# Retention state of the samples: key times value moved to ScalarE, decay and addition fused on VectorE, one more state tile

## Chip, core and metric

One core of one Trainium2 chip runs the whole program in one launch. The metric is device time in microseconds (us); three runs of the kernel before were timed, and one further execution was taken with the hardware profiler. Engines are named as in the profile: PE (TensorE), PEld (its weight loads), DVE (VectorE), ACT (ScalarE), POOL (GpSimd), SP (SyncE, which only issues transfers here).

## What is computed

One inference step of a decoder layer for 512 prompt tokens and 8 samples of one token each: RMS norm, one wide input projection, a gated MLP branch, a retention branch with 4 heads, an output projection and a feed-forward block. The change touches the retention state of the samples. Per head (key width 256, value width 512) and sample the reference computes, with c = 1 for a single token:

```
S_new = S * gamma + k^T v          # state, 256 x 512 per sample and head
o     = q S_new                    # output of the sample
```

`gamma` is one number per head, `S` comes from memory (`state_ret`) and `S_new` goes back (`new_ret_sample`).

## The kernel before

The program is one long stream of matrix products on PE. All weights come through `load_to` (line 200: quarter blocks of 256 KB, on SP's queue, three raw blocks deep), are split into a high and a low part by ACT (`wh`, line 232) and DVE (`wl`, line 234), four halves ahead of their use (`LA = 4`), and are multiplied in line 259, three products for each. Everything else is written as generators ("tasks") that advance by one step in each `micro()`; `half` calls `micro()` once for each of its four groups of six products. So the order of instructions on every engine, and of the transfers on SP's and POOL's queues, is set by this counting, and each engine works in that order.

The four heads (lines 951 to 970) each project keys, queries, values and gate, and run beside it `steps` (retention of the prompt in four chunks, lines 792 to 833: `Sh` by ACT, `Sl` by DVE, both read by PE in line 807), `o_norm` (line 777, with a power on POOL, line 784) and `samples` (line 869). `samples` works on 16 tiles per head, each 128 partitions (8 samples times 16 key rows) by 512 values:

- rows of q, k and v of the samples are copied by ACT into `srow` (tag "os", lines 879 to 884), stored by POOL to a scratch in memory (line 885) and read back spread over the partitions as `qp`, `kp` and `vp` (lines 890 to 892, POOL's queue);
- `sp_load(i)` (line 864) loads state tile i on SP's queue into one of 4 buffers; three are loaded ahead of the loop, and tile i + 3 is asked for at the end of pass i;
- pass i: ACT multiplies the tile by gamma in place (line 898); one step later DVE adds key times value (line 900) and POOL stores the result (line 901); one step later DVE adds it, weighted with the query, to `so` (lines 904, 906). A pass comes every `st["gap"]` steps, which differs by head and stage (`GAPS`).

A load into a buffer waits on SP until the store of the tile that had the buffer before has landed, and the weight loads behind it on SP's queue wait too. After the loop, `so` is split (line 910), summed over the key rows by PE (lines 913, 914), normed into `os_` (tag "os", lines 917 to 923), transposed (line 930) and added to the head's result.

The scratch tiles of `tmp()` (line 282, 4 buffers of 128 x 520) are used at the same time by the values (line 759), the gate (line 447 through `scaled`) and the branch gate `gb_task` (line 973).

Of the kernel before, what the change touches and what calls it, by code (L numbers as in the profile page):

```python
# [9 lines left out]
F32 = mybir.dt.float32  # L10
R = mybir.dt.float32r
AF = mybir.ActivationFunctionType
ALU = mybir.AluOpType
# [3 lines left out]
P = 128  # L17
DM = 1024
SEQ = 512
NS = 8  # L20
# [3 lines left out]
DV = 512  # L24
# [43 lines left out]
def trunk_kernel(ctx: ExitStack, tc: tile.TileContext, t: dict, o: dict):  # L68
# [5 lines left out]
    V, S, PE, G = nc.vector, nc.scalar, nc.tensor, nc.gpsimd  # L74
# [42 lines left out]
    def has(*keys):  # L117
        return lambda: all(k in done for k in keys)
# [154 lines left out]
    def x_tile():  # L273
        return ps_x.tile([P, 4, 128], F32, tag="x", name="xps")

    def item(label, x2, need=None, ps=None):
        ps = mm_tile() if ps is None else ps
        half(ps, label, x2, 0, True, False, need)
        half(ps, label, x2, 4, False, True, need)
        return ps  # L280

    def tmp():
        return base.tile([P, 2, HC], F32, tag="tmp", bufs=4, name="tmp")

    def tmp4():
        r = base.tile([P, 2 * HC], F32, tag="m4", bufs=2, name="tmp4")
        return r[:, :512].rearrange("p (a b) -> p a b", a=4)

    def hilo(oh, ol, src):

        S.activation(out=oh, in_=src, func=AF.Copy)
        yield
        V.tensor_tensor(out=ol, in0=src, in1=f32(oh), op=ALU.subtract)  # L293
# [69 lines left out]
    for k in range(8):  # L363
        if k in (2, 4):
# [3 lines left out]
                               op0=ALU.mult, op1=ALU.subtract)  # L368
# [15 lines left out]
    def rsqrt_mean(dst, src, scale, n=P):  # L384
        V.tensor_scalar(out=dst, in0=src, scalar1=scale, scalar2=EPS, op0=ALU.mult, op1=ALU.add)
        G.tensor_tensor(out=dst, in0=dst, in1=neghalf[:n, :dst.shape[-1]], op=ALU.pow)
# [266 lines left out]
    hp = hs.enter_context(tc.tile_pool(name="hp", bufs=1))  # L653
# [17 lines left out]
    def rope_first(ps):  # L671
        a, b = rot(), rot()
        V.tensor_tensor(out=a, in0=ps[:, :, :HC], in1=cosr, op=ALU.mult)
        V.tensor_tensor(out=b, in0=ps[:, :, :HC], in1=sinr, op=ALU.mult)  # L674
        return a, b
# [8 lines left out]
    def make_head(h):  # L684
        H = Head()
        g = gam[h]
# [176 lines left out]

        def sp_load(i):
            if i < 16:
                H.sp[i] = hp.tile([P, DV], F32, tag="sp", bufs=4, name="sp")
                nc.sync.dma_start(out=H.sp[i], in_=sview[:, :, i, :])

        def samples():

            yield has(*([("rs", h - 1)] if h else []), *[("vs", h, e) for e in range(4)])
            yield 3
            for j in range(2):
                pt = x_tile()
                for k in range(4):
                    PE.transpose(pt[:NS, k, :], H.smp[:, 4 * j + k, :], ident)
                pf = pt[:NS].rearrange("p a b -> p (a b)")
                yield
                srow = hp.tile([NS, 512], F32, tag="os", bufs=2, name="srow")
                if j == 0:  # L880
                    S.copy(out=srow[:, 0:256], in_=pf[:, 0:256])
                    S.mul(out=srow[:, 256:512], in_=pf[:, 256:512], mul=DK ** -0.5)
                else:
                    S.copy(out=srow, in_=pf)
                G.dma_start(out=row_d[h][:, 512 * j:512 * (j + 1)], in_=srow)
            qp = hp.tile([P, 16], F32, tag="qp", bufs=2, name="qp")
            kp = hp.tile([P, 16], F32, tag="kp", bufs=2, name="kp")
            vp = hp.tile([P, DV], F32, tag="vp", name="vp")
            so = hp.tile([P, DV], F32, tag="so", name="so")
            G.dma_start(out=qp, in_=row_d[h][:, 0:256].rearrange("s (b i) -> s b i", i=16))  # L890
            G.dma_start(out=kp, in_=row_d[h][:, 256:512].rearrange("s (b i) -> s b i", i=16))
            G.dma_start(out=vp, in_=row_d[h][:, 512:1024].unsqueeze(1).to_broadcast([NS, 16, DV]))
            for i in range(3):
                sp_load(i)
            yield 12
            for i in range(16):
                sp = H.sp.pop(i)
                S.mul(out=sp, in_=sp, mul=float(g))  # L898
                yield
                V.scalar_tensor_tensor(out=sp, in0=vp, scalar=kp[:, i:i + 1], in1=sp, op0=ALU.mult, op1=ALU.add)  # L900
                G.dma_start(out=oview[:, :, i, :], in_=sp)  # L901
                yield
                if i == 0:
                    V.tensor_scalar(out=so, in0=sp, scalar1=qp[:, 0:1], scalar2=None, op0=ALU.mult)
                else:
                    V.scalar_tensor_tensor(out=so, in0=sp, scalar=qp[:, i:i + 1], in1=so, op0=ALU.mult, op1=ALU.add)
                yield st["gap"] - 2
                sp_load(i + 3)
            soh, sol = (hp.tile([P, DV], R, tag=tag, bufs=n, name="so2") for tag, n in (("vp", 1), ("sp", 4)))
            yield from hilo(soh, sol, so)  # L910
            yield 11 if h == NH - 1 else 7
            po = x_tile().rearrange("p a b -> p (a b)")
            PE.matmul(po[:NS, :], lhsT=sel, rhs=soh, start=True, stop=False)
            PE.matmul(po[:NS, :], lhsT=sel, rhs=sol, start=False, stop=True)
            yield
            ss = hp.tile([P, 1], F32, tag="ss", bufs=2, name="ss_s")
            os_ = hp.tile([NS, DV], F32, tag="os", bufs=2, name="os_")
            S.activation(out=os_, in_=po[:NS], func=AF.Square, accum_out=ss[:NS])
            S.copy(out=os_, in_=po[:NS])
            yield 3  # L920
            rsqrt_mean(ss[:NS], ss[:NS], 1.0 / DV, NS)
            yield 2
            S.activation(out=os_, in_=os_, func=AF.Copy, scale=ss[:NS])
            yield has(*[("r", h, e) for e in range(4)])
            yield
            rh, rl = rT[h]
            pt = x_tile()
            pv = pt[:, 0, :32].rearrange("p (e s) -> p e s", e=4)
            for e in range(4):
                PE.transpose(pv[:, e, :], os_[:, 128 * e:128 * (e + 1)], ident[:NS, :NS])  # L930
            yield
            rs = tmp4()[:, 0, :32].rearrange("p (e s) -> p e s", e=4)
            for hh in range(2):
                z = rs[:, :, 4 * hh:4 * hh + 4]
                V.tensor_tensor(out=z, in0=pv[:, :, 4 * hh:4 * hh + 4], in1=H.sgs[:, :, hh], op=ALU.mult)
            yield
            for hh in range(2):
                yield from hilo(rh[:, :, hh, 256:HC], rl[:, :, hh, 256:HC], rs[:, :, 4 * hh:4 * hh + 4])
            done.add(("rs", h))
# [11 lines left out]
    for h in range(NH):  # L951
        H = make_head(h)
        st["gap"] = GAPS[h][0]
        a, b = rope_first(item(f"k{h}_0", X))
# [3 lines left out]
        a, b = rope_first(item(f"q{h}_0", X))  # L958
# [395 lines left out]
```

## Time and profile before

| | us |
|---|---|
| three timed runs | 1127.29, 1132.49, 1132.52 |
| their median | 1132.49 |
| the profiled execution, its own time | 1129.06 |
| its span, first to last instruction | 1127.3 |
| PE busy in the span | 1106.0 (98%) |
| DVE busy | 774.0 (69%) |
| ACT busy | 544.6 (48%) |
| POOL busy | 90.0 (8%) |
| granted TensorE clock, mean over the span | 0.996 of full |

How to read it: the profiled execution's time exceeds its span by 1.8 us, which lies outside of the instructions. PE's busy share counts time in which a product is under way; what is left, about 21 us, holds the start, the end and the waits between. The views used below are the page's list of engines, who waited for whom, instructions in order of time, groups of instructions by line and shape, and busy times in given windows.

### The profile page before, as it was taken

How to read it: one execution, taken by the hardware profiler on the slowest of the kernel's cores; microseconds unless marked ns; L12 is line 12 of the kernel's file. 1: busy time of each engine (PE TensorE's matmuls, PEld its weight loads, DVE VectorE, ACT ScalarE, POOL GpSimd, SP SyncE). 2: the span in 40 equal slices, each digit the busy share in tenths (PEclk: the TensorE clock that was granted, in tenths of full speed). 3: DMA queues.
4: the chain of work that ended last, by engine and by line, in shares of the span. 5: the costliest groups of instructions: out<-in, count | busy, mean ns of one | idle time of the engine just before them, and what ended most of it. 6: DMA issues, size and time to landing. Idle time of an engine off the chain costs nothing.

```text
span 1127.3 us, 22375 instructions
## 1 busy us (share of the span) xinstructions
PE 1106.0 (98%) x8954; PEld 1085.4 (96%) x8954; DVE 774.0 (69%) x1384; ACT 544.6 (48%) x999; POOL 90.0 (8%) x148
## 2 busy tenths in 40 slices
PE   9999999999999999999999999999999999999996
PEld 8999999999999899999998999999999999999996
DVE  6567833464895379557864877769868767767765
ACT  6465523245555544554455444456544444544541
POOL 0100000001211111111012121000000000000000
PEclk9999999999999999999999999999999999999998
DMA  8423243431666078428561686652323323323302
GB/s 294 132 76 95 80 129 98 128 103 50 165 200 207 21 201 248 143 51 229 153 196 38 199 269 219 189 170 76 113 76 113 113 76 113 109 80 103 99 25 76
DMA packets 112616, 148.08 MB, mean 131 GB/s; under 512 B 13752, under 2 KB 81528, under 8 KB 112512
## 3 DMA queue, kind: packets, MB, share of 16 engines
q1 hardware_dynamic: 97696, 118.75, 34.2%
q0 software_dynamic: 12336, 24.72, 7.7%
q10 hardware_dynamic: 2480, 3.19, 0.8%
q8 instruction: 70, 1.15, 0.4%
q14 instruction: 34, 0.28, 0.1%
HBM read 121.16 MB, written 25.43 MB: 130 GB/s over the span
## 4 chain that ended last, share of the span: by engine, by line
PE 81%; issue 5%; DVE 5%; DMA 4%; ACT 2%; POOL 1%; SPq 0%; ACTq 0%; DVEq 0%; POOLq 0%
PE mm L259 58%; PE bA L1171 6%; PE bB L1171 4%; PE xps L807 2%; PE bD L1171 2%; PE bC L1171 2%; PE st_ps L813 2%; DMA sp<-in_state_ret 1%; DMA raw<-in_w_in 1%; DVE wl L234 1%; PE mm L1142 1%; DVE sp L900 1%; PE xps L771 1%; ACT wh L232 1%; PE bA L1282 1%
## 5 line engine op out<-in xcount | busy, mean ns | idle before, releaser
L232 ACT ACTIVATE wh<-raw 128x512 fp32r<-128x512 f32 x333 | 209.6, 631 | 296.6 <-PE mm L259 233.5
L234 DVE TENSOR_TENSOR wl<-raw,wh 128x512 fp32r<-128x512 f32 x333 | 228.3, 687 | 95.0 <-ACT wh L232 94.0
L259 PE MATMUL mm<-xh,wh 128*128 128x260 f32 x1264 | 260.7, 287 | 2.9 <-DVE rot L674 1.2
L259 PE MATMUL mm<-xl,wh 128*128 128x260 f32 x1264 | 254.2, 283 | 0.3 <-DVE xl L367 0.3
L259 PE MATMUL mm<-xh,wl 128*128 128x260 f32 x1264 | 254.2, 283 | 0.0
L259 PEld LDWEIGHTS mm<-xh,wh 128*128 128x128 f32 x1264 | 195.7, 189 | 6.9 <-ACT wh L232 1.4
L259 PEld LDWEIGHTS mm<-xl,wh 128*128 128x128 f32 x1264 | 194.6, 188 | 0.6 <-DVE xl L367 0.5
L259 PEld LDWEIGHTS mm<-xh,wl 128*128 128x128 f32 x1264 | 194.7, 188 | 0.0
L259 PE MATMUL mm<-ah,wh 128*128 128x260 f32 x576 | 116.0, 283 | 0.0
L259 PE MATMUL mm<-al,wh 128*128 128x260 f32 x576 | 115.9, 283 | 0.0
L259 PE MATMUL mm<-ah,wl 128*128 128x260 f32 x576 | 115.7, 282 | 0.0
L259 PEld LDWEIGHTS mm<-ah,wl 128*128 128x128 f32 x576 | 88.8, 188 | 0.0
L259 PEld LDWEIGHTS mm<-al,wh 128*128 128x128 f32 x576 | 88.7, 188 | 0.1
L259 PEld LDWEIGHTS mm<-ah,wh 128*128 128x128 f32 x576 | 88.5, 188 | 0.0
L1179 DVE TENSOR_TENSOR x<-x,mm 128x520 f32<-128x520 f32 x56 | 38.8, 694 | 37.9 <-PE mm L259 37.9
L900 DVE SCALAR_TENSOR_TENSOR sp<-vp,kp,sp 128x512 f32<-128x512 f32 x64 | 47.8, 747 | 15.5 <-ACT sp L898 15.4
L901 POOL DMA_DIRECT2D out_new_s<-sp x64 | 39.0, 610 | 224.8 <-DVE sp L900 211.5
L234 DVE TENSOR_TENSOR wl<-sums,wh 128x512 fp32r<-128x512 f32 x60 | 41.3, 689 | 19.8 <-ACT wh L232 19.3
L232 ACT ACTIVATE wh<-sums 128x512 fp32r<-128x512 f32 x60 | 37.7, 629 | 33.6 <-PE mm L259 28.2
L259 PE MATMUL mm<-rl,wh 128*128 128x260 f32 x256 | 52.0, 284 | 0.6 <-DVE rl L293 0.6
L447 DVE TENSOR_TENSOR tmp<-mm,rb 128x520 f32<-128x520 f32 x37 | 25.8, 697 | 38.6 <-PE mm L259 38.6
L259 PE MATMUL mm<-rh,wh 128*128 128x260 f32 x256 | 51.6, 283 | 0.3 <-DVE ld L1007 0.3
(362 smaller groups left out, 2161.8 us busy)
## 6 DMA issues: line engine op xcount, KB each, us to landing
raw<-in_w_in SPq DMA_DIRECT2D x158, 256.0 KB
sp<-in_state_ret SPq DMA_DIRECT2D x64, 256.0 KB
out_new_s<-sp POOLq DMA_DIRECT2D x64, 256.0 KB, 5.6
raw<-in_w_up SPq DMA_DIRECT2D x64, 256.0 KB
raw<-in_w_down SPq DMA_DIRECT2D x64, 256.0 KB
raw<-in_w_proj_ret SPq DMA_DIRECT2D x32, 256.0 KB
raw<-in_w_proj_gm SPq DMA_DIRECT2D x16, 256.0 KB
raw<-in_w_out SPq DMA_DIRECT2D x16, 256.0 KB
```

Of the source, the lines that this page charges most:

```text
L232: S.activation(out=wh, in_=src, func=AF.Copy)
L234: V.tensor_tensor(out=wl, in0=src, in1=f32(wh), op=ALU.subtract)
L259: PE.matmul(ps[:, hh, :HC], lhsT=w[:, j, :], rhs=x[:, k, hh, :], start=(first and q == 0), stop=(last and q == 2))
L447: V.tensor_tensor(out=z, in0=ps[:, :, :HC], in1=rb, op=ALU.mult)
L771: PE.transpose(pt[:, c, :], z[:, hh, off:off + 128], ident)
L807: PE.matmul(po, lhsT=a, rhs=b, start=(n == 0), stop=(n == len(mms) - 1))
L813: PE.matmul(st_ps[:, d, :], lhsT=a[:, c, ks], rhs=b[:, c, :], start=(c == 0 and n == 0), stop=(c == 3 and n == 2), skip_group_check=True)
L900: V.scalar_tensor_tensor(out=sp, in0=vp, scalar=kp[:, i:i + 1], in1=sp, op0=ALU.mult, op1=ALU.add)
L901: G.dma_start(out=oview[:, :, i, :], in_=sp)
L1142: PE.matmul(ps[:, hh, :HC], lhsT=w[:, j, :], rhs=x[:, j, 2 * kh + hh], start=(kh + j + n == 0), stop=(kh == 1 and j == 3 and n == 2))
L1171: PE.matmul(ps, lhsT=w[:, k, :], rhs=x, start=(first and k + n == 0), stop=(k == 3 and n == 2), skip_group_check=True)
L1179: V.tensor_tensor(out=x1[:, m], in0=x1[:, m], in1=ps[:, :, :HC], op=ALU.add)
```

## The change

In each of the 64 passes ACT now computes key times value into a scratch tile `kv` from `tmp()` (scale `kp[:, i:i+1]`, one value per partition), without touching the state tile; DVE then does decay and addition in one operation on the loaded tile, with gamma as an immediate. The state tiles get 5 buffers in place of 4; the tiles with tag "os" get 1 in place of 2.

```diff
         def sp_load(i):
             if i < 16:
-                H.sp[i] = hp.tile([P, DV], F32, tag="sp", bufs=4, name="sp")
+                H.sp[i] = hp.tile([P, DV], F32, tag="sp", bufs=5, name="sp")
...
-                srow = hp.tile([NS, 512], F32, tag="os", bufs=2, name="srow")
+                srow = hp.tile([NS, 512], F32, tag="os", bufs=1, name="srow")
...
             for i in range(16):
+                kv = tmp()[:, :, 0:256]
+                S.activation(out=kv, in_=vp.rearrange("p (a b) -> p a b", a=2), func=AF.Copy, scale=kp[:, i:i + 1])
+                yield
                 sp = H.sp.pop(i)
-                S.mul(out=sp, in_=sp, mul=float(g))
-                yield
-                V.scalar_tensor_tensor(out=sp, in0=vp, scalar=kp[:, i:i + 1], in1=sp, op0=ALU.mult, op1=ALU.add)
+                V.scalar_tensor_tensor(out=sp, in0=sp, scalar=float(g), in1=kv, op0=ALU.mult, op1=ALU.add)
...
-            soh, sol = (hp.tile([P, DV], R, tag=tag, bufs=n, name="so2") for tag, n in (("vp", 1), ("sp", 4)))
+            soh, sol = (hp.tile([P, DV], R, tag=tag, bufs=n, name="so2") for tag, n in (("vp", 1), ("sp", 5)))
...
-            os_ = hp.tile([NS, DV], F32, tag="os", bufs=2, name="os_")
+            os_ = hp.tile([NS, DV], F32, tag="os", bufs=1, name="os_")
```

Every engine keeps its instructions in the same places; what changes is the operands and what each instruction waits for. The first place is ACT in the second head (head 1), the first passes over the state. Names in brackets are semaphores: DMAHW those of transfers from SP's queue, DMASW those from POOL's. Before:

```order
L898 ACTIVATE sp<-sp 128x512 [waits DMAHW3_49,DMASW6_49]
L898 ACTIVATE sp<-sp 128x512 [waits DMAHW4_49,DMASW7_49]
L947 COPY pbacc<-mm 128x520 [waits PE_49]
L232 ACTIVATE wh<-raw 128x512 [waits DMAHW7_49,DMAHW6_49]
L898 ACTIVATE sp<-sp 128x512 [waits DMAHW5_49,DMASW0_49]
L947 COPY pbacc<-mm 128x520 [waits PE_49]
L232 ACTIVATE wh<-raw 128x512
L898 ACTIVATE sp<-sp 128x512 [waits DMAHW0_49,DMASW5_49]
```

And now, at the same place:

```order
L898 ACTIVATE tmp<-vp,kp 128x2x256 [waits DMASW5_49,DMASW4_49]
L898 ACTIVATE tmp<-vp,kp 128x2x256
L948 COPY pbacc<-mm 128x520 [waits PE_49]
L232 ACTIVATE wh<-raw 128x512 [waits DMAHW7_49,DMAHW6_49]
L898 ACTIVATE tmp<-vp,kp 128x2x256
L948 COPY pbacc<-mm 128x520 [waits PE_49]
L232 ACTIVATE wh<-raw 128x512
L898 ACTIVATE tmp<-vp,kp 128x2x256
```

ACT's operation of the pass waited for the load of its state tile (DMAHW); now only the first of a head waits, for `vp` and `kp`. The wait for the load stands at DVE's operation of the pass (line 901 of the new program).

The second place is SP's queue in the same head: the first loads of state tiles among the weight loads. Before, and then now:

```order
L867 DMA sp<-in_state_ret 128x1x512 [waits DMAHW0_49,DMASW5_49,PE_49]
L200 DMA raw<-in_w_in 128x2x256 [waits DMAHW1_49,DVE_49]
L200 DMA raw<-in_w_in 128x2x256 [waits DMAHW2_49]
L867 DMA sp<-in_state_ret 128x1x512 [waits DMAHW3_49,DMASW7_49,DVE_49]
L200 DMA raw<-in_w_in 128x2x256 [waits DMAHW4_49]
L867 DMA sp<-in_state_ret 128x1x512 [waits DMAHW5_49,DMASW0_49,DVE_49]
```

```order
L867 DMA sp<-in_state_ret 128x1x512 [waits DMAHW0_49,DMASW0_49]
L200 DMA raw<-in_w_in 128x2x256 [waits DMAHW1_49,DVE_49]
L200 DMA raw<-in_w_in 128x2x256 [waits DMAHW2_49]
L867 DMA sp<-in_state_ret 128x1x512 [waits DMAHW3_49,DMASW4_49,PE_49]
L200 DMA raw<-in_w_in 128x2x256 [waits DMAHW4_49]
L867 DMA sp<-in_state_ret 128x1x512 [waits DMAHW5_49,DMASW7_49,DVE_49]
```

These are the loads of tiles 3, 4 and 5. Tile 4 waited for the store of this head's tile 0 (DMASW7); now tile 5 does, and tile 4 waits only for what the head before left.

The third place is ACT in the third head (head 2), where the second row is copied into the one buffer that is left:

```order
 L882 ACTIVATE srow<-xps 8x256
-L884 COPY srow<-xps 8x512 [waits PE_49,Activation_49]
+L884 COPY srow<-xps 8x512 [waits DMASW0_49,PE_49,Activation_49]
```

The copy now also waits until the store of the first row has landed (DMASW0); the same stands in the other heads.

## Rows read from the trace of the kernel before

**Rows 1.** The page: busy time of PE (us, share of the span, instructions), and the shares of the chain that ended last, by engine.

```profile
PE 1106.0 (98%) x8954; PEld 1085.4 (96%) x8954; DVE 774.0 (69%) x1384; ACT 544.6 (48%) x999; POOL 90.0 (8%) x148
PE 81%; issue 5%; DVE 5%; DMA 4%; ACT 2%; POOL 1%; SPq 0%; ACTq 0%; DVEq 0%; POOLq 0%
```

**Rows 2.** Who PE waited for, whole span: us in total, times, longest us.

```profile
PE xps L807 <- DVE Sl L824: 1.7, 1, 1.7
PE xps L913 <- ACT wh L232: 1.3, 1, 1.3
PE xps L930 <- ACT os__8296 L923: 1.2, 1, 1.2
PE mm L259 <- DVE rot L674: 1.2, 1, 1.2
...
PE mm L259 <- DVE tmp L447: 0.5, 1, 0.5
```

**Rows 3.** Windows of 6 us in head 1: stretch, then busy us (and instructions) of PE, PEld, DVE, ACT, POOL, then granted clock, DMA share, GB/s.

```profile
390.00:396.00 6.00, 6.00 (x52) 6.00 (x52) 3.61 (x6) 4.03 (x8) 1.78 (x3) 1.00 0.22 55
...
402.00:408.00 6.00, 6.00 (x53) 6.00 (x52) 1.50 (x2) 0.80 (x2) 0.61 (x1) 1.00 0.79 261
...
426.00:432.00 6.00, 4.80 (x40) 4.62 (x39) 6.00 (x10) 3.21 (x6) 0.60 (x1) 1.00 0.92 257
...
450.00:456.00 6.00, 4.85 (x42) 4.64 (x40) 5.91 (x12) 3.12 (x7) 1.03 (x2) 1.00 0.58 189
```

**Rows 4.** ACT in order of time, head 1, its operation of passes 4 and 5: start us, us, what, [idle before it, and who ended it].

```profile
403.70 0.63 ACT L898 ACTIVATE sp<-sp 128x512 f32<-128x512 f32 x1 [3.10 <-DMA sp<-in_state_ret]
407.83 0.63 ACT L898 ACTIVATE sp<-sp 128x512 f32<-128x512 f32 x1 [3.50 <-DMA sp<-in_state_ret]
```

**Rows 5.** DVE in order of time, the same stretch: its operation of passes 4, 5 and 9, and the evacuation that PE waited for at 428 us.

```profile
404.37 0.75 DVE L900 SCALAR_TENSOR_TENSOR sp<-vp,kp,sp 128x512 f32<-128x512 f32 x1 [3.03 <-ACT sp L898]
...
408.50 0.75 DVE L900 SCALAR_TENSOR_TENSOR sp<-vp,kp,sp 128x512 f32<-128x512 f32 x1 [2.59 <-ACT sp L898]
...
421.71 0.75 DVE L900 SCALAR_TENSOR_TENSOR sp<-vp,kp,sp 128x512 f32<-128x512 f32 x1 [0.77 <-ACT sp L898]
...
428.48 0.69 DVE L674 TENSOR_TENSOR rot<-mm,sinr 128x520 f32<-128x520 f32 x1
```

**Rows 6.** SP's queue in order of time: the last weight loads before the loop of head 1, and the loads of state tiles 4 and 5.

```profile
361.07 0.89 SPq L200 DMA_DIRECT2D raw<-in_w_in  x2
397.88 0.62 SPq L867 DMA_DIRECT2D sp<-in_state_ret  x1
...
399.60 0.63 SPq L867 DMA_DIRECT2D sp<-in_state_ret  x1
```

**Rows 7.** POOL in order of time: the store of state tile 0 of head 1.

```profile
393.68 0.64 POOL L901 DMA_DIRECT2D out_new_s<-sp  x1 [3.16 <-DVE sp L900]
```

**Rows 8.** Waits over the whole span, of SP's queue, of ACT and of DVE: us in total, times, longest us.

```profile
SPq L867 <- DMA out_new_s<-sp: 256.0, 50, 35.9
ACT sp L898 <- DMA sp<-in_state_ret: 23.8, 13, 4.8
DVE sp L900 <- ACT sp L898: 15.4, 10, 3.3
```

**Rows 9.** Groups of instructions by line and shape: count | busy us, mean ns of one | idle before. The first two are the operations of the pass, the third is ACT with a scale per partition from SBUF to SBUF, the last is DVE's same operation with an immediate in place of a value per partition.

```profile
L900 DVE SCALAR_TENSOR_TENSOR sp<-vp,kp,sp 128x512 f32<-128x512 f32 x64 | 47.8, 747 | 15.5 <-ACT sp L898 15.4
L898 ACT ACTIVATE sp<-sp 128x512 f32<-128x512 f32 x64 | 39.6, 621 | 23.8 <-DMA sp<-in_state_ret 23.8
L788 ACT ACTIVATE ob<-ob,ss 128x512 f32<-128x512 f32 x14 | 10.0, 715 | 0.0
L1123 DVE SCALAR_TENSOR_TENSOR tmp<-tmp,rb 128x520 f32<-128x520 f32 x30 | 20.8, 694 | 0.0
```

**Rows 10.** Around PE's wait on `Sl` in head 1: POOL's store of the first row, ACT's copy of the second and POOL's load of `vp`, in order of time, and the window in which PE waited (columns as in Rows 3).

```profile
370.37 0.59 POOL L885 DMA_DIRECT2D row_d<-srow  x1 [5.35 <-ACT srow L882]
374.76 0.56 ACT L884 COPY srow<-xps 8x512 f32<-8x512 f32 x1
379.64 0.59 POOL L892 DMA_DIRECT2D vp<-row_d  x1 [2.23 <-issue]
380.00:400.00 20.00, 18.20 (x125) 16.84 (x125) 10.61 (x18) 12.09 (x24) 4.42 (x8) 0.91 0.23 59
```

**Rows 11.** The same place in head 2, in order of time: POOL's store of the first row, ACT's copy of the second, POOL's load of `vp`, DVE's second half of `Sl`, and PE's product that reads it; and the least, median and largest time from issue to landing of the stores of line 885.

```profile
475.28 0.59 POOL L885 DMA_DIRECT2D row_d<-srow  x1 [14.91 <-ACT srow L882]
475.56 0.58 ACT L884 COPY srow<-xps 8x512 f32<-8x512 f32 x1 [0.56 <-PE xps L876]
480.31 0.59 POOL L892 DMA_DIRECT2D vp<-row_d  x1 [1.65 <-PE st_ps L813]
483.07 0.69 DVE L824 SCALAR_TENSOR_TENSOR Sl<-st_ps,Sh 128x512 fp32r<-128x512 f32 x1 [0.67 <-ACT Sh L822]
485.67 0.40 PE L807 MATMUL xps<-Sl,q 128*128 128x512 f32 x1
DMA to landing us min/median/max: 1.8/1.9/3.5
```

**Rows 12.** The end of the last head's samples: ACT in order of time, and the window around it (columns as in Rows 3).

```profile
682.17 0.63 ACT L232 ACTIVATE wh<-raw 128x512 fp32r<-128x512 f32 x1 [1.21 <-DMA raw<-in_w_proj_ret]
679.00:685.00 6.00, 6.00 (x51) 5.80 (x49) 5.14 (x10) 3.21 (x6) 1.33 (x1) 1.00 0.96 362
```

## Prediction, before the changed kernel was run

> **What bounds the kernel now.** I read the page first. PE is busy for 1106.0 of 1127.3 us and makes up 81% of the chain [rows 1], so no edit on ACT or DVE pays for itself; it can only give back time in which PE stands still, about 21 us with the start and the end. Next the list of whom PE waits for: in the part with the four heads the waits are few and short, 1.7, 1.3, 1.2, 1.2 and 0.5 us [rows 2]. That is the whole stake of this change, and the rest of the reading asks which of these waits hang on the samples' state.
>
> Three of them do, by way of DVE. In head 1 the passes over the state come closest together. ACT sits for 3.10 and 3.50 us before its operation in passes 4 and 5, each time until the state tile has landed [rows 4]; DVE, which comes after ACT in the pass, then sits idle for 3.03 and 2.59, and once more 0.77 in pass 9, 6.4 us in all [rows 5]. Between 402 and 408 us DVE is busy for only 1.50 of 6 us; afterwards it works off a backlog, 6.00 of 6 us busy from 426 to 432, where PE loses 1.2, and 5.91 from 450 to 456, where PE loses another 1.15 [rows 3]. The evacuation that PE waited for at 428 us starts at 428.48, with no idle time before it [rows 5]: DVE is late, not held up there. So PE's waits on `tmp` (0.5), `rot` (1.2) and, through the split weights, on `wh` (1.3) are the bill for DVE's idle time 20 to 50 us earlier: 3.0 us [rows 2].
>
> Why were the tiles late? SP's queue stands still from 361.96 to 397.88 us, on the load of tile 4 [rows 6]. The store of tile 0 was issued at 393.68 [rows 7], so it took 4.2 us until SP could go on. The load of tile 4, issued at 397.88, holds ACT until 403.70 (5.8 us), that of tile 5, issued at 399.60, until 407.83 (8.2 us) [rows 4, 6]. Such waits of SP on stores sum to 256.0 us in 50 cases, the longest 35.9 [rows 8]. Meanwhile the transfer engines idle: DMA share 0.22 from 390 to 396, 0.79 and more afterwards [rows 3].
>
> **The change, part by part.**
>
> *Fifth buffer.* Tile 4 of a head no longer waits for a store of the same head. In head 1 its load goes out in SP's idle stretch, and DVE's 3.03 us go. Tile 5 then waits for the store of tile 0 and goes out at about 397.9 in place of 399.6. If it needs the same 8.2 us it lands at 406.1; DVE, now 3.0 us earlier, is ready for it at about 402.9 (408.50 - 2.59 - 3.0 [rows 5]), and waits 3.2 us. DVE's idle time falls from 6.4 to between 3.2 and 4.0, so DVE gets to its backlog 2.4 to 3.2 us earlier. Each of the three waits of PE (0.5, 1.2, 1.3) is shorter than that, so I take all three off: **-3.0 us**. The bounds are 0 (the loads land no earlier) and -3.0.
>
> *Who waits for the load.* ACT's 23.8 us in 13 waits [rows 8] end. The load is now awaited by DVE, and behind it on DVE stand weight splits and evacuations; but DVE waited for ACT in the same place already (15.4 us in 10 cases [rows 8]), and the tile no longer has to pass through 0.62 us of ACT first. Nothing new is behind the wait: 0 us.
>
> *Durations.* ACT's operation gets a scale per partition; the nearest row takes 715 ns against 621, so 64 x 0.094 = 6.0 us more of ACT. DVE's gets an immediate; the nearest row takes 694 ns for 520 values against 747 for 512, so 64 x 0.053 = 3.4 us less of DVE [rows 9]. ACT is 48% busy [rows 1] and loses its waits; its cover is the four weight halves split ahead. Head 1 has 16 of the 64 passes, 0.8 us less of DVE in the backlog, which only secures the first term. On PE: 0.
>
> *Scratch tiles.* 64 more tiles go through the 4 buffers of `tmp()`. ACT may now wait for DVE to have read the `kv` of some passes before. In the branch gate's stage a buffer can also be held until a 260 KB tile is stored, but ACT has stood for up to 4.8 us on a state tile [rows 8], and of PE's waits on ACT none exceeds 1.3 [rows 2]. 0 us, nothing to gain, bounded above by the next item.
>
> *One row buffer.* The copy of the second row waits for the store of the first. That store, issued at 475.28 in head 2, needs 1.8 to 1.9 us [rows 11], so the copy moves from 475.56 to about 477.15, 1.6 us. Behind it on POOL come the second store, the loads of `qp`, `kp`, `vp` and then a power that DVE waits for ahead of `Sl`. DVE's second half of `Sl` ends at 483.07 + 0.69 = 483.8, and PE's product that reads it starts at 485.67: slack 1.9 us, 0.3 more than the delay [rows 11]. In head 1 exactly this chain already costs the wait of 1.7 us on `Sl` [rows 2], after which the granted clock fell to its lower level (mean 0.91 over 20 us, so 20 x 0.09 = 1.8 us lost) [rows 10]; there the copy starts 4.4 us behind the issue of the first store and does not move. Likeliest 0; bounds 0 and +3.5 (one more such event, 1.7 + 1.8).
>
> *The end.* In the last head PE's 1.2 us on `os_` follow a weight block that landed 1.21 us late, in a window with a DMA share of 0.96 [rows 2, 12]. SP gets to that block earlier, but the transfer engines are full. Bounds 0 and -1.2; I take **-0.5**, nearer to nothing, because of the full engines.
>
> *Sum:* -3.0 - 0.5 = **-3.5 us**, or 1129.06 - 3.5 = 1125.6 for the profiled execution. That execution lies 3.4 us below the median of the runs (1132.49), and the four executions known (1127.29, 1129.06, 1132.49, 1132.52) show two levels that nothing here explains. I apply the sum to their middle, (1129.06 + 1132.49) / 2 = 1130.8, and forecast **1127.3 us**, 0.46% below the median. About 0.5%, 5.7 us, is what a measurement of this kernel can tell from no change: under 1126.8 would be faster, over 1138.2 slower.
>
> A rule that speaks against the largest term: the Trainium skill, "DMA: Bandwidth & Descriptors", section "Issuing engines are not separate DMA queues", says that all transfers run on the same 16 engines and interleave, whoever issues them. By that rule a load issued 1.7 us earlier into a share of 0.79 to 0.92 lands hardly earlier; the trace agrees in that the load of tile 5 took longer than that of tile 4. By the rule alone the sum would be near 0; by the rows it is -3.5, since tile 4's load moves into the idle stretch.
>
> **Rivals.**
>
> *A. The forecast*, DVE earlier in head 1: 1127.3, own range 1123 to 1132. For it: the idle time stands right ahead of the backlog.
>
> *B. The transfers bind.* Stores and loads of 512 KB per pass beside the weights keep the engines at 0.8 to 0.9 [rows 3]; loads are issued earlier and land when they did. Then DVE's idle time only moves, and the time stays at 1130.8. Against it: the share of 0.22 before the loop, into which one load per head fits. The rule of the Trainium skill named above would make it this case.
>
> *C. More comes back.* Also the 1.2 us at the end and the event of head 1 (1.7 + 1.8 [rows 2, 10]) go, because transfers are spread better: 3.0 + 1.2 + 3.5 = 7.7 less, 1123.1. Against it: that event hangs on POOL's `vp` load, which the change does not touch; for it: the 3 to 5 us between the runs may be such events.
>
> *D. The row buffer makes it slower.* If in heads 0 and 2 the store of the row takes over 0.3 us longer than its median (3.5 is the maximum shown [rows 11]), the chain behind it misses its slack, PE waits and the clock falls, as in head 1: 2 x (1.7 + 1.8) = 7.0 more. With nothing gained elsewhere that is 1132.49 + 7.0 = 1139.5, slower. Against it: both heads need to miss it, on top of no gain.
>
> That the change doesn't do what it says can be left out: the waits stand in the order of instructions.
>
> **How the numbers follow.** A 0.53, B 0.20, C 0.17, D 0.10. A lies just above the line of 1126.8, so I give 0.20 of it to faster and 0.33 to no difference; with C, faster is 0.37; with B, no difference is 0.53; slower is D, 0.10. The range reaches from C's side, 1121.5, to 1134.0, which is B at the higher of the two levels; D and the far end of C are left out.
>
> **What would show it.** Right: ACT has no wait on a state load; DVE's waits at line 901 in head 1 sum to under 4.5 us; PE's waits from 410 to 460 us sum to under 0.8 where they were 3.0; SP does not stand still on tile 4 but on tile 5. B: DVE idle there for 6 us as before, with the same waits of PE. D: a wait of PE for `Sl` of over 1 us in head 0 or 2, and a granted clock under 1.00 there. Wrong altogether would be a new wait of PE of over 2 us that ends on ACT's `kv` or on a scratch tile.

## The result, and the profile of the changed kernel

The changed kernel takes 1121.49 us (median of 12 runs, 1118.84 to 1124.08); the kernel before, timed beside it, 1127.45 (12 runs, 1124.95 to 1132.52). The ratio is 0.9944, 95% interval 0.9926 to 0.9961: 6.3 us off 1127.45 by the ratio (4.4 to 8.3 by the interval), 6.0 by the medians. So the gain is real, but whether it exceeds the 0.5% that the prediction drew as its line, the interval leaves open. The forecast was 1127.3 with a range from 1121.5 to 1134.0; the result lies 5.8 us below the forecast and 0.01 us below the range.

The profiled executions are 1129.06 us (span 1127.3) and 1121.07 us (span 1119.4). The page of the changed kernel, busy time of the engines and the shares of the chain that ended last:

```profile
PE 1103.7 (99%) x8954; PEld 1084.0 (97%) x8954; DVE 770.4 (69%) x1384; ACT 549.8 (49%) x999; POOL 88.3 (8%) x148
...
PE 94%; issue 2%; DVE 2%; DMA 1%; ACT 1%; POOL 0%; SPq 0%; ACTq 0%; DVEq 0%; POOLq 0%
```

Against [rows 1], PE's busy time fell by 2.3 us and its idle time from 21.3 to 15.7, by 5.6: together the 7.9 us between the spans. The 2.3 are not fewer products. They are mostly the stretch that ran before at the lower clock, 1.8 us [rows 10]. Whom PE waits for now, whole span (us in total, times, longest us):

```profile
PE bB L1237 <- DVE dg L1232: 2.4, 1, 2.4
PE mm L259 <- ACT xh L366: 1.2, 1, 1.2
PE ps_w L344 <- DVE ones L337: 1.1, 1, 1.1
PE xps L876 <- ACT ob L781: 0.7, 1, 0.7
```

All five waits of [rows 2], on `Sl`, `wh`, `os_`, `rot` and `tmp`, 5.9 us, are gone; what heads the list lies at the end, at the start and between heads. (From line 900 of the kernel before on, the changed kernel's numbers are one higher.) Head 1 by windows, columns as in [rows 3], first the four stretches shown there, then the one of [rows 10]:

```profile
390.00:396.00 6.00, 6.00 (x52) 6.00 (x52) 5.35 (x10) 4.35 (x9) 1.85 (x3) 1.00 0.38 86
402.00:408.00 6.00, 6.00 (x53) 6.00 (x52) 3.94 (x8) 1.95 (x4) 1.20 (x2) 1.00 0.83 252
426.00:432.00 6.00, 6.00 (x53) 6.00 (x52) 5.96 (x12) 3.63 (x6) 0.60 (x1) 1.00 0.94 260
450.00:456.00 6.00, 6.00 (x52) 5.96 (x51) 3.44 (x9) 5.20 (x12) 0.56 (x1) 1.00 0.80 234
380.00:400.00 20.00, 19.86 (x149) 18.40 (x148) 12.09 (x21) 14.45 (x27) 4.46 (x8) 1.00 0.34 90
```

PE is busy for 6.00 of 6 in each of the four. DVE does 3.94 us of work from 402 to 408 where it did 1.50, and is through with its backlog by 450 (3.44 where it was 5.91). The last row has the full clock and no wait on `Sl`. SP's queue in the changed kernel, the load of tile 4, then of tiles 5 and 6, and behind them DVE's operation of the pass, passes 4, 5 and 6:

```profile
362.80 0.62 SPq L867 DMA_DIRECT2D sp<-in_state_ret  x1
...
395.35 0.63 SPq L867 DMA_DIRECT2D sp<-in_state_ret  x1
...
397.06 0.63 SPq L867 DMA_DIRECT2D sp<-in_state_ret  x1
```

```profile
398.74 0.69 DVE L901 SCALAR_TENSOR_TENSOR sp<-sp,tmp 128x512 f32<-128x512 f32 x1
...
401.34 0.69 DVE L901 SCALAR_TENSOR_TENSOR sp<-sp,tmp 128x512 f32<-128x512 f32 x1 [1.11 <-DMA sp<-in_state_ret]
...
405.36 0.69 DVE L901 SCALAR_TENSOR_TENSOR sp<-sp,tmp 128x512 f32<-128x512 f32 x1 [2.06 <-DMA sp<-in_state_ret]
```

Tile 4 is asked for 35 us earlier than in [rows 6], in SP's idle stretch, and pass 4 finds it there; SP now stands still on tile 5. Passes 5 and 6 still wait, 3.2 us in all where three passes waited 6.4 [rows 5]. Who waits over the whole span, and the two operations of the pass by line and shape (columns as in [rows 8, 9]):

```profile
SPq L867 <- DMA out_new_s<-sp: 225.4, 43, 31.4
...
ACT srow L884 <- DMA row_d<-srow: 7.2, 2, 3.9
...
DVE sp L901 <- ACT tmp L898: 4.8, 5, 1.9
...
DVE sp L901 <- DMA sp<-in_state_ret: 3.2, 2, 2.1
...
ACT tmp L898 <- DMA gb_d<-tmp: 2.5, 1, 2.5
```

```profile
L898 ACT ACTIVATE tmp<-vp,kp 128x512 f32<-128x512 f32 x64 | 45.3, 711 | 2.5 <-DMA gb_d<-tmp 2.5
...
L901 DVE SCALAR_TENSOR_TENSOR sp<-sp,tmp 128x512 f32<-128x512 f32 x64 | 43.8, 685 | 8.1 <-ACT tmp L898 4.8 <-DMA sp<-in_state_ret 3.2
```

ACT waits for no state load any more, once for a scratch tile (2.5 us) and twice for the row buffer (7.2); none of these reaches PE.

The last head, which the prediction gave one short paragraph, shows the same picture as head 1. The kernel before, DVE in order of time:

```profile
657.34 0.75 DVE L900 SCALAR_TENSOR_TENSOR sp<-vp,kp,sp 128x512 f32<-128x512 f32 x1 [1.26 <-ACT sp L898]
...
663.25 0.75 DVE L900 SCALAR_TENSOR_TENSOR sp<-vp,kp,sp 128x512 f32<-128x512 f32 x1 [3.29 <-ACT sp L898]
...
673.11 0.75 DVE L900 SCALAR_TENSOR_TENSOR sp<-vp,kp,sp 128x512 f32<-128x512 f32 x1 [1.30 <-ACT sp L898]
```

That is 5.9 us of DVE's time lost to late state tiles, 12 to 28 us ahead of PE's wait at 685.4 us. In the changed kernel no pass of this head waits for a load; the two that wait at all wait for ACT (3.3 us). Where the DMA share of 0.96 stood [rows 12], the changed kernel has:

```profile
679.00:685.00 6.00, 6.00 (x51) 6.00 (x52) 3.62 (x9) 2.10 (x5) 0.73 (x2) 1.00 0.31 98
```

The program is about 7 us ahead by then, and the last state load goes out 11.2 us earlier (654.22 against 665.44), so the transfers are done some 4 us earlier against PE's work as well.

### The profile page after: what moved, and what is told of

Its sections match the earlier page's. It is cut to its first block, busy times and chain, and to the rows that moved or that the text cites. A ratio compares the mean times of both kernels' runs of the same rounds, so it can differ in the third digit from the quotient of the medians.

```text
span 1119.4 us, 22317 instructions
## 1 busy us (share of the span) xinstructions
PE 1103.7 (99%) x8954; PEld 1084.0 (97%) x8954; DVE 770.4 (69%) x1384; ACT 549.8 (49%) x999; POOL 88.3 (8%) x148
## 4 chain that ended last, share of the span: by engine, by line
PE 94%; issue 2%; DVE 2%; DMA 1%; ACT 1%; POOL 0%; SPq 0%; ACTq 0%; DVEq 0%; POOLq 0%
PE mm L259 69%; PE bA L1172 6%; PE bB L1172 4%; PE xps L807 2%; PE bD L1172 2%; PE bC L1172 2%; PE st_ps L813 2%; PE mm L1143 1%; PE xps L771 1%; PE xps L853 1%; DMA xT<-in_xT 1%; PE bA L1283 1%; PE ps_v L259 1%; DVE x L1251 0%; PE bB L1283 0%
## 5 line engine op out<-in xcount | busy, mean ns | idle before, releaser
L259 PE MATMUL mm<-rh,wl 128*128 128x260 f32 x256 | 51.5, 282 | 0.0
```

What stands on the lines that cost most here:

```text
L259: PE.matmul(ps[:, hh, :HC], lhsT=w[:, j, :], rhs=x[:, k, hh, :], start=(first and q == 0), stop=(last and q == 2))
```

## Experiments

Every kernel below was timed side by side with the kernel before, on one chip, and its ratio is to that; experiments 7 and 8 are single profiled executions.

### 1. The fifth tile alone

```diff
-                H.sp[i] = hp.tile([P, DV], F32, tag="sp", bufs=4, name="sp")
+                H.sp[i] = hp.tile([P, DV], F32, tag="sp", bufs=5, name="sp")
-                srow = hp.tile([NS, 512], F32, tag="os", bufs=2, name="srow")
+                srow = hp.tile([NS, 512], F32, tag="os", bufs=1, name="srow")
...
```

> The kernel before with 5 state tiles and one row buffer, its operations as before (ACT scales the state tile in place, DVE adds key times value). Theory 'buffers' (the waits of PE in head 1 come from the slot cycle of store and load): 3 to 5 us faster than before, DVE's idle time ahead of line 900 from 390 to 460 us falls from 6.4 to about 3.5, and PE's waits there from 3.0 to under 0.8. Theory 'ACT freed' (what counted is that ACT no longer stands on a state load): within 1.5 us of before, PE's waits there still over 2.

Measured: 1120.68 us (1119.47 to 1123.52), ratio 0.9946 [0.9931, 0.9961], the same as the whole change. Waits over the span:

```profile
ACT sp L898 <- DMA sp<-in_state_ret: 12.5, 6, 3.1
...
DVE sp L900 <- ACT sp L898: 7.6, 9, 1.5
```

Against [rows 8] ACT's wait on loads is halved, DVE's too (2.9 us of it in head 1, where it was 6.4), and of PE's five waits none is left. So the buffers bring the whole gain, as far as the intervals can tell. Five tiles with two row buffers were not tried: the second row buffer is the space that the fifth tile takes, 512 values in each partition.

### 2. The operations alone

```diff
             for i in range(16):
+                kv = tmp()[:, :, 0:256]
+                S.activation(out=kv, in_=vp.rearrange("p (a b) -> p a b", a=2), func=AF.Copy, scale=kp[:, i:i + 1])
+                yield
                 sp = H.sp.pop(i)
-                S.mul(out=sp, in_=sp, mul=float(g))
-                yield
-                V.scalar_tensor_tensor(out=sp, in0=vp, scalar=kp[:, i:i + 1], in1=sp, op0=ALU.mult, op1=ALU.add)
+                V.scalar_tensor_tensor(out=sp, in0=sp, scalar=float(g), in1=kv, op0=ALU.mult, op1=ALU.add)
```

> The new operations alone (ACT key times value into scratch, DVE decay and addition), with 4 state tiles and two row buffers as before. 'Buffers': within 1.5 us of before, DVE now idle itself on the loads of tiles 4 and 5 for 5 us or more in all, PE's waits in head 1 at 2 us or more. 'ACT freed': 3 us or more faster, PE's waits there under 0.8.

Measured: 1125.53 us (1122.32 to 1129.69), ratio 0.9992 [0.9978, 1.0007], no difference. DVE now waits for the loads itself, 6.3 us in head 1, and PE still waits there for `rot` and at line 914, 1.8 us in all (I had expected 2 or more). The profiled execution has no wait on `Sl`. Waits over the span, of DVE and then of PE:

```profile
DVE sp L901 <- DMA sp<-in_state_ret: 12.9, 7, 2.3
```

```profile
PE xps L914 <- DVE tmp L747: 1.0, 1, 1.0
PE mm L259 <- DVE rot L674: 0.8, 1, 0.8
```

Moving the wait from ACT to DVE, the longer operation on ACT and the shorter one on DVE are together worth nothing that shows: between 2.5 us less and 0.8 more, by the interval.

### 3. The row buffer alone

```diff
-                srow = hp.tile([NS, 512], F32, tag="os", bufs=2, name="srow")
+                srow = hp.tile([NS, 512], F32, tag="os", bufs=1, name="srow")
...
-            os_ = hp.tile([NS, DV], F32, tag="os", bufs=2, name="os_")
+            os_ = hp.tile([NS, DV], F32, tag="os", bufs=1, name="os_")
```

> The kernel before with one row buffer in place of two, nothing else. If the row buffer is hidden, as predicted: within 1.5 us of before, ACT's second row copy 1.6 us later in heads 0 and 2 and no new wait of PE. If it costs: a wait of PE for Sl of over 1 us in head 0 or 2 and 3.5 us more. If it was what freed the second row's store (which landed in 3.5 us before and in 1.8 after): the second store lands in 1.8 us in all heads, the wait of 1.7 us on Sl in head 1 is gone, and 3 us less.

Measured: 1127.27 us (1124.64 to 1133.29), ratio 0.9998 [0.9984, 1.0012], no difference. ACT does wait for the row's store (4.7 us in 2 cases), and no wait of PE on `Sl` follows in heads 0 and 2. The profiled execution was the longest of them, and it shows what a long execution with four tiles consists of. Windows of 20 us in it, columns as in [rows 3], and PE's waits:

```profile
380.00:400.00 20.00, 18.12 (x123) 16.43 (x122) 10.14 (x18) 11.66 (x22) 4.18 (x7) 0.91 0.22 57
420.00:440.00 20.00, 17.00 (x133) 16.82 (x132) 16.07 (x29) 8.48 (x16) 2.26 (x4) 0.91 0.77 223
680.00:700.00 20.00, 18.32 (x140) 17.87 (x139) 11.27 (x23) 7.94 (x17) 4.24 (x5) 0.91 0.57 209
```

```profile
PE mm L259 <- DVE rot L674: 3.0, 1, 3.0
...
PE xps L807 <- DVE Sl L824: 1.7, 1, 1.7
PE xps L930 <- ACT os__8296 L923: 1.7, 1, 1.7
```

The same three places as in [rows 2], two of them longer, and each followed by a lower clock (0.91 over 20 us, 1.8 us lost each).

### 4. The load of `vp` six steps later, kernel before

```diff
-            G.dma_start(out=vp, in_=row_d[h][:, 512:1024].unsqueeze(1).to_broadcast([NS, 16, DV]))
...
-            yield 12
+            yield 6
+            G.dma_start(out=vp, in_=row_d[h][:, 512:1024].unsqueeze(1).to_broadcast([NS, 16, DV]))
+            yield 6
```

POOL's load of `vp` waits for the store of the second row, and a power that `Sl` needs stands behind it. Asked for later, the load stands behind that power, which then no longer waits for the store.

> The kernel before with the load of vp asked for 6 steps later, so that the power of the head's normalization stands ahead of it on POOL. If PE's wait on Sl in head 1 and the fall of the clock behind it (1.7 + 1.8 us) are there in most runs of the kernel before: about 3 us faster and no wait on Sl. If they were an accident of the one profiled execution: within 1 us of before.

Measured: 1123.42 us (1122.70 to 1125.36), ratio 0.9975 [0.9965, 0.9984]: some 3 us, and the runs lie within 2.7 us where those of the kernel before beside it lie within 5.4. The wait on `Sl` and the lower clock are gone; those of head 1 on late tiles remain, 3.0 us (of `tmp` below, 1.0 is in head 1 and 0.3 in the last head):

```profile
PE xps L914 <- ACT wh L232: 1.3, 1, 1.3
PE mm L259 <- DVE tmp L447: 1.3, 3, 0.6
...
PE mm L259 <- DVE rot L674: 0.7, 1, 0.7
```

So the wait on `Sl` can go while the tiles come as late as before: DVE still loses 7.0 us to them in head 1. The gain and the narrower spread speak for a wait that is in most runs of the kernel before. They do not give its price alone, because the last head cost 0.3 us in this execution and 1.2 and 1.9 in the two profiles of the kernel before [rows 2, experiment 7].

### 5. The same in the changed kernel

> The changed kernel, with the load of vp asked for 6 steps later (as in the experiment on the kernel before that gained 0.25%). The question is whether the fifth buffer itself removes PE's wait on Sl in head 1 with the clock fall behind it (3 to 3.5 us), or whether the changed kernel still has it in part of its runs and only the profiled ones were spared. Theory S (the buffer removes it): same as the changed kernel, ratio 0.9935 to 0.9955. Theory H (a matter of each run, when the second row's store takes 3.5 us and not 1.8): the mean gain adds, 1 to 3 us below the changed kernel, ratio 0.991 to 0.9935, with a narrower spread of the runs.

Measured: 1119.26 us (1119.04 to 1119.60), ratio 0.9942 [0.9928, 0.9957]. The ratio is S's; the spread, 0.6 us where the changed kernel has 5, is H's. By the ratios of the changed kernel (0.9944 in the result, 0.9951 in experiment 9) 0.2 to 1 us is left to gain. The wider spread suggests that some runs of the changed kernel still have a wait that this edit takes away. The edit is that of experiment 4.

### 6. The dose: three tiles

```diff
-                H.sp[i] = hp.tile([P, DV], F32, tag="sp", bufs=4, name="sp")
+                H.sp[i] = hp.tile([P, DV], F32, tag="sp", bufs=3, name="sp")
...
```

> The kernel before with three state tiles in place of four (old operations, two row buffers): the dose in the other direction. Theory 'buffers' (a load that waits for a store of its own head comes too late, DVE idles early in head 1 and PE waits at its backlog): DVE's idle time on late state tiles in head 1 grows from 6.4 to 9 us or more, PE's waits from 410 to 460 us from 3.0 to 5 or more, and one of them is long enough (1.7 or more) for a clock fall; 3 to 9 us slower, ratio 1.003 to 1.008. Theory 'transfers bind' (loads land when the transfer engines get to them, however early they are issued): no difference, ratio 0.999 to 1.001.

Measured: 1164.05 us (1155.64 to 1168.89), ratio 1.0333 [1.0299, 1.0367], 38 us slower: right in sign and four times what I allowed. Waits over the span, of SP's queue, ACT and DVE, then PE's longest:

```profile
SPq L867 <- DMA out_new_s<-sp: 311.8, 50, 42.2
...
ACT sp L898 <- DMA sp<-in_state_ret: 67.9, 25, 7.9
DVE sp L900 <- ACT sp L898: 53.2, 23, 6.5
```

```profile
PE mm L259 <- DVE tmp L447: 11.7, 4, 6.4
PE xps L771 <- DVE tmp L747: 8.5, 3, 4.1
PE mm L259 <- DVE rot L674: 5.0, 1, 5.0
PE mm L259 <- ACT pbacc L947: 3.6, 1, 3.6
```

With 3, 4 and 5 tiles DVE idles 53.2, 15.4 [rows 8] and 7.6 us (experiment 1) in passes whose tile is late: the load cannot go out before a store of its own head has landed, and each tile less makes that wait come earlier. PE's idle time grew by 24.7 us (46.0 against 21.3), and its busy time by 9.2 (1115.2 against 1106.0), with a mean clock of 0.984 where it was 0.996. I had priced head 1 alone; but DVE loses 17.5 us in head 1 and 17.5 in the last head, and there PE waits for 13.1 us: 10.7 on `tmp` between 677 and 708 us, and 2.4 at line 771.

### 7 and 8. Both kernels profiled once more

> The kernel before, unchanged, profiled once more: which of its waits are there in every execution. Theory 'the loads' says that the waits of head 1 on tmp, rot and wh (together 3.0 us) come back within 0.5 us, and that the wait on Sl and the one at the end vary with how long a small store or a weight block takes. Rival: all five vary alike.

> The changed kernel, unchanged, profiled once more. Theory S (the buffer removes the wait on Sl): no wait of PE over 0.6 us from 370 to 460 us, no window with a granted clock under 1.00 there. Theory H (each run by itself): with a second row's store of 3.5 us in head 1 a wait on Sl of 1.5 us or more, with one of 1.8 us none.

Measured: 1128.31 and 1120.28 us. PE's waits in the kernel before that belong to this story:

```profile
PE mm L259 <- DVE tmp L447: 2.7, 2, 1.9
...
PE xps L807 <- DVE Sl L824: 1.7, 1, 1.7
PE xps L913 <- ACT wh L232: 1.2, 1, 1.2
...
PE mm L259 <- ACT sp L898: 0.8, 1, 0.8
```

Head 1 costs 2.8 us again (0.8, 0.8 and 1.2), though one of the three waits has another name; the wait on `Sl` is there again; and the last head costs 1.9, now on `tmp` at 673 us and not on `os_`. What PE waits for changes from one execution to the other; where DVE idles on late tiles does not: 7.5 us in head 1 (6.4 in [rows 5]) and 8.3 in the last head (5.9 in the first profile). The changed kernel has none of these waits again. Its second row's store landed in 1.9 us, so this execution cannot tell theory S from theory H.

### 9 and 10. The changed kernel beside the best of both

> The changed kernel, unchanged, timed beside its variant with the later vp load and beside the kernel before. If the fifth buffer's kernels rarely have the wait on Sl of head 1 (one row store slowed by an instruction fetch), the median is within 1.0 us of the variant's and most runs lie within 3 us; ratio 0.993 to 0.996. If they have it in half of their runs or more, the median is 1.5 to 3.5 us above the variant's.

> The old operations with the fifth state tile, one row buffer and the later vp load: what the trace points to as enough. If the new operations are worth nothing, the same as the changed kernel with the later vp load: 1118.5 to 1120.5 us, ratio 0.992 to 0.995, runs within 2 us. If ACT's freedom from the state loads is worth something once the other waits are gone, 1 us or more slower than that.

Measured: 1120.22 us (1119.71 to 1125.71), ratio 0.9951 [0.9935, 0.9967], for the changed kernel; 1120.01 (1119.42 to 1121.24), ratio 0.9943 [0.9928, 0.9958], for the old operations with five tiles and the later load. The medians are 0.2 us apart, and experiment 5, the variant that the expectation means, lies 1.0 below, timed on another chip: most runs of the changed kernel, it seems, have no wait on `Sl`; none of its three profiles has one. Six of its eight runs lie within 1.2 us, the other two 3.8 and 6.0 us above the lowest. Of its 20 timed runs, here and in the result, six took 1123.4 us or more, at a mean granted clock of 0.993 to 0.995, and the other 14 at most 1122.5, at 0.996 or 0.997. So a lower clock comes in a minority of them. Whether it follows a wait on `Sl` in head 1 or one in head 2 that comes by the one row buffer, no profile shows, since none fell on such a run. The old operations do as well as the new ones, so ACT's freedom from the loads is worth nothing that shows, even when the other waits are gone.

## Why the prediction was wrong

The forecast lies 5.8 us above the result: 3.3 of that are the base to which the sum was applied, and 2.5 the sum itself, -3.5 where the medians moved by 6.0. In the sum the term of the fifth buffer held. Two steps failed: the end was priced at -0.5 because full transfer engines would hold the gain back, and the wait on `Sl` with the lower clock was put at nothing. PE's waits and the lower clock, term by term, in the two pairs of profiles, the second being experiments 7 and 8 (us taken off):

| term | predicted | first pair | second pair |
|---|---|---|---|
| head 1, late tiles | 3.0 | 3.0 | 2.8 |
| last head | 0.5 | 1.2 | 1.9 |
| wait on `Sl` in head 1 | 0 | 1.7 | 1.7 |
| lower clock after it | 0 | 1.8 | 0 |
| sum | 3.5 | 7.7 | 6.4 |
| difference of the spans | | 7.9 | 8.0 |

The second pair leaves 1.6 us outside of the table. Nearly all of it is busy time of PE, 1105.2 us before and 1103.7 after, with the full clock in all four heads of both; what shortened it was not found.

**The base.** The sum was applied to 1130.8, the middle of four executions. The 64 timed runs of the kernel before, in four sets, have medians of 1126.3 to 1127.5, and two of my four (1132.49 and 1132.52) are the highest of them all. From 1127.45 the sum of -3.5 would have given 1123.9, 2.5 us above the result. The forecast was 0.46% below the median that I knew, and 0.56% was measured; that these come close is luck, since 1.7 of the 5.2 us forecast were the step from one base to another.

**Fifth buffer, -3.0: right, in cause and size.** DVE's idle time on late tiles in head 1 fell to 3.2 us, the forecast's lower end, and the three waits of PE (3.0 us in the profiled execution, 2.8 in the second) are gone. Passes 5 and 6 share what I gave to pass 5. Experiment 1 shows that the buffer does it, experiment 6 that it goes by the number of tiles.

**Who waits, durations, scratch tiles: 0, right.** ACT's operation takes 711 ns (715 estimated), DVE's 685 (694), and experiment 2 measures all of it as 0.9992 [0.9978, 1.0007]. ACT's one wait for a scratch tile, 2.5 us, is hidden.

**One row buffer: 0, right in the time, with nothing to spare.** Experiment 3: 0.9998 [0.9984, 1.0012]. In head 2 of the changed kernel the first row's store took 3.5 us and not the 1.9 I had counted with, so ACT's copy came at 472.53 with 3.86 us of waiting; but the second store landed in 1.8, so the delay of the loads behind them stayed near 1.7. That used up the slack of 1.9 us. The second half of `Sl` ends at 479.16, and PE's product reads it 0.14 us later, in order of time:

```profile
478.47 0.69 DVE L824 SCALAR_TENSOR_TENSOR Sl<-st_ps,Sh 128x512 fp32r<-128x512 f32 x1 [0.66 <-ACT Sh L822]
479.30 0.42 PE L807 MATMUL xps<-Sl,q 128*128 128x512 f32 x1
```

Rival D's mechanism began and just missed PE. Experiment 3 could not show it: with four tiles that store took 1.8 us, and in the six executions profiled with five tiles 2.9 to 3.8. Why is not known.

**The end, -0.5: the step that failed by its reasoning.** I read a weight block landing 1.21 us late beside a DMA share of 0.96, and concluded that full transfer engines would hold the gain back. The share was a sign of work caught up late, not of a limit: the last state load had waited on SP until 665, the weights and states behind came in a bunch, and DVE had lost 5.9 us to late tiles just before. With a fifth tile the transfers are spread forward, the share at that place is 0.31, and the whole wait goes: 1.2 us in one pair of profiles, 1.9 in the other. The number of tiles decides it: with three, DVE loses 17.5 us in the last head and PE waits for 13.1; in five executions profiled with four, DVE loses 5.7 to 8.3 and PE 0.3 to 1.9; in six with five, 3.1 to 4.0 and PE nothing. The 0.3 and 0.5 of experiments 4 and 2 show that the size of -0.5 was possible; the reason given for it was wrong. I had seen the mechanism in head 1 and did not seek it in the last head, where DVE's waits at line 900 show it.

**The wait on `Sl` and the clock behind it: left at 0 and failed, worth 3.5 us in the first pair of profiles and 1.7 in the second.** Rival C held 3.0 + 1.2 + 3.5 = 7.7 us, and the first pair shows these: 5.9 us of waits and 1.8 of clock. To the 7.9 between the spans, 1.2 go off for longer waits at the start (`xh` 1.2, it was 0.4, and one of 0.4 on `vtok`), and 1.4 come on: 0.9 in stops of 0.3 us or less and 0.5 of PE's busy time. I gave C 0.17, because POOL's load of `vp` is untouched by the change. Experiment 4 fits that argument, as it removes this wait without a fifth tile. Yet in the changed kernel the load went out at 378.66, 7.5 us behind the first row's store at 371.11, where it had been 9.3 [rows 10], because the second row's store landed in 1.8 us and not in 3.5. Experiment 9 suggests that this is the usual case there. **Why the store is quick with five tiles stays open**: the kernels with `vp` in its old place had it at 1.8 to 1.9 us in all four executions profiled with five tiles in the changed kernel or experiment 1, and at 3.3 to 3.6 in four of five with fewer tiles (experiment 2 is the fifth, 1.9). With the later load, behind which the power no longer stands, it was 1.8 in experiments 4 and 5 and 3.4 in experiment 10, five tiles, without harm. It is not the number of tiles by itself.

**Rival B** fell: the engines were not full. From 400 to 420 us they moved 224 GB/s before and 264 after (first line before, second after; columns as in [rows 3]), and the load asked for 35 us earlier was there:

```profile
400.00:420.00 20.00, 19.47 (x163) 19.08 (x161) 13.44 (x22) 8.12 (x15) 3.62 (x7) 1.00 0.75 224
400.00:420.00 20.00, 20.00 (x171) 20.00 (x169) 16.82 (x30) 10.74 (x19) 3.37 (x7) 1.00 0.87 264
```

The Trainium skill's page "DMA: Bandwidth & Descriptors", section "Issuing engines are not separate DMA queues", says that transfers run on the same 16 engines and interleave, whichever engine started them. Nothing here speaks against it; but that the sum would be near 0 did not follow from it, with a share of 0.75.

The list of what would show the forecast right was met in each point; it could not have told A from C, since it did not ask for the last head or the clock.

## What to carry to other kernels

If a buffer's reload waits for a store of the same stage, count the buffers it needs, not the engine time of the operation between: one tile of 256 KB was worth as much as the whole change, one tile less cost 38 us. When a wait is traced back to idle time of another engine, look for that idle time in every stage that runs the same loop before pricing the rest by other causes; and take a high DMA share for a limit only if the queue did not stand still shortly before it.

## What the runs showed of the hardware

- **A wait does not settle the clock.** Waits of PE of 1.7, 3.0 and 1.7 us in experiment 3 and of 1.7 in the first profile were each followed by the lower clock (0.91 of full over 20 us, that is some time at 1.2 and not at 2.4 GHz). In the second profile of the kernel before, waits of 1.7 and 1.9 us were not, so the 1.7 us that the expectation of experiment 6 took for long enough is no bound:

```profile
380.00:400.00 20.00, 18.14 (x136) 16.75 (x135) 11.15 (x19) 12.70 (x24) 5.37 (x9) 1.00 0.27 71
660.00:680.00 20.00, 18.07 (x149) 17.67 (x148) 15.90 (x26) 9.42 (x16) 4.81 (x9) 1.00 0.98 317
```

- **The store of the second row in head 1, 16 KB, takes 1.8 to 1.9 or 3.3 to 3.6 us on nearly idle transfer engines** (DMA share 0.12 and 0.06 in the two stretches of 2 us from 376 us on, in the first profile of the kernel before, where it took 3.5). In each execution of every kernel here one transfer of instructions (16 KB, 0.9 to 1.3 us) runs beside the second row's store of head 1. By the trace's packet records it began 1.27 to 1.39 us after the store's issue in the five executions where the store took the longer time, and 1.37 to 1.45 after in the seven where it took the shorter. The two groups overlap between 1.37 and 1.39, so the order of the two is a hint and no more; that the one transfer holds up the other was not tried.
